# Row sums of 64 MB: seven rows of the last group moved to the head of the load stream

## The chip, the cores and the metric

One core of one Trainium2 chip runs the kernel. The metric is device time in microseconds, the median of several executions. Every execution here is fast, at a granted clock of 1.0. A profile's span is some 2 us shorter than the device time of the same execution, so spans are compared with spans and times with times.

Words and names used below: a load is *issued* when the sync engine starts it and *lands* when the last mark of its completion has come; an instruction that waits for it starts about 0.02 us later in these profiles. In the lines shown, DVE is the vector engine and ACT the scalar engine, SPq is the sync engine's queue, TENSOR_REDUCE is a reduction, CUSTOM_DVE_ANT_0 a halving (both are explained with the kernel), and ACTIVATE the sum of one row on ACT.

## The reference

```python
batch, seq, dim = 32, 512, 1024
x = np.random.randn(batch, seq, dim).astype(np.float32)      # 67.1 MB
return np.sum(x, axis=-1).astype(np.float32)                  # 16,384 sums
```

Each of the 16,384 rows of 1,024 numbers is added up. There is one addition for every number read, so the question is how fast 67.1 MB come in, and how little is left to do when the last of them has come.

## The kernel before

The 16,384 rows are laid out as 8 groups of 128 partitions by 16 rows; one group is 8 MB (8 x 2^20 bytes, 8.39 million), 64 KB for each partition. Three buffers of one group rotate. All loads are issued by the sync engine, in order, on one queue. `vec` is one reduction over several rows on the vector engine; `halves` adds the first half of one row to its second half and accumulates the sum, also on the vector engine; `act` sums one row on ACT. `hold` keeps a load from being issued until a given instruction is done; here the load of group 1 waits for the first sum.

```python
last = J // BIG - 1          # 7
FIRST = 4
pieces = (560, 464)
# ... tc.tile_pool(name="in", bufs=3) as inpool; vec, hold, halves, act: cut ...

def rows(t, a, n, j, n_act, pairs=False):      # load n rows, nv on the vector engine, the rest on ACT
    nv = n - n_act
    block = t[:, a * dim : (a + n) * dim].rearrange("p (n d) -> p n d", d=dim)
    load = nc.sync.dma_start(out=block, in_=rows_from(j, n))
    if pairs:
        for q in range(nv):
            sums_of.append(halves(sums[:, j + q : j + q + 1], block[:, q, :]))
    else:
        sums_of.append(vec(sums[:, j : j + nv], block[:, :nv, :]))
    for q in range(nv, n):
        act(sums[:, j + q : j + q + 1], block[:, q, :], dim)
    return load

for g in range(last):
    t = inpool.tile([P, BIG * dim + 4], fp32)
    if g == 0:
        rows(t, 0, FIRST, 0, 0)
        first = sums_of[-1]
        rows(t, FIRST, BIG - FIRST, FIRST, 0)
        continue
    load = rows(t, 0, BIG, g * BIG, BIG // 2 if g == last - 1 else 0)
    if g == 1:
        hold(load, first, "no descriptors of later loads while the first ones start")

t = inpool.tile([P, BIG * dim + 4], fp32)
j = last * BIG
rows(t, 0, 8, j, 4)
rows(t, 8, 5, j + 8, 2, pairs=True)
two = rows(t, 13, 2, j + 13, 1, pairs=True)
a = BIG - 1
# ... the last row: a clear, two loads of 560 and 464 columns, a halving after each ...
```

The sum of the first piece of the last row is put into the tile beside the second piece, so the last halving has 466 numbers left (464, the sum, and a zero).

## Time and profile before

| kernel before | value |
|---|---|
| device time, median of 3 | 161.72 us (161.71 to 161.91) |
| span of the profiled execution | 160.2 us |
| vector engine busy | 120.1 us, 75% |
| ACT busy | 17.3 us, 11% |
| loads in the stream | 13 |
| mean spacing of whole groups' landings | 19.42 us |

The prediction below shows the chain, the stretches and the end. Two more views are wanted. The first is the page's queue part: queue and kind, packets, MB, and the time of the packets as a share of 16 engines' span.

```profile
q1 hardware_dynamic: 2016, 67.12, 97.7%
```

The second view is the timeline of the last 4 us: start, length, engine, line, operation, shapes, and in brackets how long the engine was idle before it and for what.

```profile
154.11 0.69 DVE L145 CUSTOM_DVE_ANT_0 t<-t 128x512 f32<-128x512 f32 x1 [1.68 <-DMA t<-in_x_dram]
...
156.62 0.69 DVE L145 CUSTOM_DVE_ANT_0 t<-t 128x512 f32<-128x512 f32 x1 [0.59 <-DMA t<-in_x_dram]
156.62 1.03 ACT L158 ACTIVATE unread<-t 128x1024 f32<-128x1024 f32 x1 [0.32 <-DMA t<-in_x_dram]
...
157.37 0.45 DVE L145 CUSTOM_DVE_ANT_0 t<-t 128x280 f32<-128x280 f32 x1
...
157.97 0.40 DVE L145 CUSTOM_DVE_ANT_0 t<-t 128x233 f32<-128x233 f32 x1
```

At 156.62 both engines start on the two-row piece, which has just landed, and both have been waiting for it, the vector engine for 0.59 us.

### The profile page before, as it was taken

The numbers are of one execution on the slowest core, as the hardware profiler recorded it, in microseconds if no ns is written. First come the engines' busy times: TensorE is split into PE (matmuls) and PEld (weight loads), VectorE is DVE, ScalarE is ACT, GpSimd is POOL, SyncE is SP. The second block draws the span as 40 slices with busy tenths as digits, with TensorE's granted clock in tenths as the row PEclk, the third lists the DMA queues.
The fourth block names the chain that finished last, engine by engine and source line by source line (L and its number), as shares of the span: only waits on it lengthen the run. The fifth ranks groups of instructions, "written<-read, shape, count | busy, mean of one in ns | idle before, by whom it ended". The sixth has DMA issues, their size and how long they took to land.

```text
span 160.2 us, 125 instructions
## 1 busy us (share of the span) xinstructions
DVE 120.1 (75%) x22; ACT 17.3 (11%) x31; POOL 0.2 (0%) x4
## 2 busy tenths in 40 slices
DVE  0190059960799959999499994999949999497953
ACT  3000000000000000000000000000000000496953
POOL 0000000000000000000000000000000000000000
DMA  7999996996996996989969969969969969899994
GB/s 270 450 479 503 393 524 262 523 523 262 524 523 262 523 524 262 523 360 425 524 262 523 523 262 524 523 262 523 523 262 523 507 278 523 376 409 410 424 382 109
DMA packets 2928, 67.18 MB, mean 419 GB/s; under 512 B 1264, under 2 KB 1392, under 8 KB 1520
## 3 DMA queue, kind: packets, MB, share of 16 engines
q1 hardware_dynamic: 2016, 67.12, 97.7%
q10 hardware_dynamic: 912, 0.06, 0.3%
HBM read 67.11 MB, written 0.07 MB: 419 GB/s over the span
## 4 chain that ended last, share of the span: by engine, by line
DMA 73%; DVE 25%; SPq 1%; issue 0%; DVEq 0%
DMA t<-in_x_dram 73%; DVE sums L131 24%; SPq L170 1%; SPq L211 0%; DVE t L145 0%; DVEq L242 0%
## 5 line engine op out<-in xcount | busy, mean ns | idle before, releaser
L131 DVE TENSOR_REDUCE sums<-t 128x16 f32<-128x16384 f32 (+3 forms) x9 | 116.6, 12953 | 35.9 <-DMA t<-in_x_dram 35.9
L158 ACT ACTIVATE unread<-t 128x1024 f32<-128x1024 f32 x15 | 15.2, 1012 | 139.7 <-DMA t<-in_x_dram 139.7
L145 DVE CUSTOM_DVE_ANT_0 t<-t 128x512 f32<-128x512 f32 (+2 forms) x6 | 3.5, 602 | 2.4 <-DMA t<-in_x_dram 2.3
L158 ACT ACTIVATION_READ_ACCUMULATOR unread<-t 128x1 f32 x15 | 2.8, 187 | 0.0
L158 ACT ACT_TABLE_LOAD x1 | 1.3, 1283 | 0.8 <-PEq L231 0.8
L145 DVE DVE_READ_ACCUMULATOR2_ANT sums<- 128x1 f32 x5 | 0.4, 83 | 0.0
L231 POOL MEMSET const-bfloat16-1.0<- 128x1 bf16 x1 | 0.1, 101 | 0.0
L231 POOL MEMSET const-uint8-127<- 128x1 uint8 x1 | 0.1, 101 | 0.0
L231 POOL MEMSET const-float32-0.0<- 128x1 f32 x1 | 0.1, 98 | 0.2 <-issue 0.2
L231 POOL MEMSET const-float32-1.0<- 128x1 f32 x1 | 0.1, 98 | 0.0
L145 DVE DVE_READ_ACCUMULATOR2_ANT t<- 128x1 f32 x1 | 0.1, 83 | 0.0
L209 DVE MEMSET t<- 128x1 f32 x1 | 0.1, 59 | 0.0
## 6 DMA issues: line engine op xcount, KB each, us to landing
t<-in_x_dram SPq DMA_DIRECT2D x1, 6144.0 KB, 21.0
t<-in_x_dram SPq DMA_DIRECT2D x1, 4096.0 KB, 31.2
t<-in_x_dram SPq DMA_DIRECT2D x1, 2560.0 KB, 37.0
t<-in_x_dram SPq DMA_DIRECT2D x1, 2048.0 KB, 7.2
t<-in_x_dram SPq DMA_DIRECT2D x1, 1024.0 KB, 39.0
t<-in_x_dram SPq DMA_DIRECT2D x1, 280.0 KB, 39.2
t<-in_x_dram SPq DMA_DIRECT2D x1, 232.0 KB, 39.3
t<-in_x_dram SPq DMA_DIRECT2D x6, 41.1
```

The source lines that it names most:

```text
L131: return nc.vector.tensor_reduce(out=dst, in_=src, axis=mybir.AxisListType.X, op=mybir.AluOpType.add)
L145: return nc.vector.tensor_tensor_reduce(out=src[:, :n], in0=src[:, :n], in1=src[:, n:], scale=1.0, scalar=0.0, op0=mybir.AluOpType.add, op ...
L158: nc.scalar.activation(out=unread[:, :n], in_=src, func=mybir.ActivationFunctionType.Copy, accum_out=dst,)
L170: load = nc.sync.dma_start(out=block, in_=rows_from(j, n))
L209: nc.vector.memset(whole[:, width + 1 :], 0.0)
L231: nc = _bacc.Bacc("TRN2", target_bir_lowering=False, num_devices=1)
```

## The change

Before, the last group arrives after everything else, and its 16 rows are worked off in pieces of 8, 5, 2 and 1. The change moves 7 of these rows to the very start of the stream, where the vector engine has nothing to do, and leaves 9 for the end, in pieces of 6, 2 and 1. Group 0 is loaded whole. In group 6, the last whole group, nine rows are halved on the vector engine and seven summed by ACT, instead of eight reduced and eight summed.

```diff
-    FIRST = 4
+    FIRST = 7
...
+        j = last * BIG
+        t = inpool.tile([P, BIG * dim + 4], fp32)
+        rows(t, 0, FIRST, j, 0)
+        first = sums_of[-1]
         for g in range(last):
             t = inpool.tile([P, BIG * dim + 4], fp32)
-            if g == 0:
-                rows(t, 0, FIRST, 0, 0)
-                first = sums_of[-1]
-                rows(t, FIRST, BIG - FIRST, FIRST, 0)
-                continue
-            load = rows(t, 0, BIG, g * BIG, BIG // 2 if g == last - 1 else 0)
+            if g < last - 1:
+                load = rows(t, 0, BIG, g * BIG, 0)
+            else:
+                rows(t, 0, BIG, g * BIG, 7, pairs=True)
             if g == 1:
                 hold(load, first, "no descriptors of later loads while the first ones start")

         t = inpool.tile([P, BIG * dim + 4], fp32)
-        j = last * BIG
-        rows(t, 0, 8, j, 4)
-        rows(t, 8, 5, j + 8, 2, pairs=True)
-        two = rows(t, 13, 2, j + 13, 1, pairs=True)
+        rows(t, FIRST, 6, j + FIRST, 2, pairs=True)
+        two = rows(t, FIRST + 6, 2, j + FIRST + 6, 1, pairs=True)
```

## The prediction

> **What bounds the kernel now.** I read the page's chain of work that ended last first, because it says which engine a saved microsecond must come from.
>
> ```profile
> ## 4 chain that ended last, share of the span: by engine, by line
> DMA 73%; DVE 25%; SPq 1%; issue 0%; DVEq 0%
> ```
>
> 73% is the load stream and 25% is the vector engine. The vector share looks like a second limit, but the chain only runs through the reductions at the points where a later load waits for a buffer (three buffers rotate). Whether that wait stops the stream is read from how evenly the loads land. So the second view is the table by stretches, cut at the moments when each reduction starts, which are the landings. Its columns are the stretch and its length, then busy time and count for the vector engine, ACT and POOL, the clock, the DMA share and GB/s.
>
> ```profile
> 7.25:21.78 14.53, 4.42 (x2) 0.00 (x0) 0.00 (x0) 1.00 1.04 451
> 21.78:41.14 19.36, 12.95 (x2) 0.00 (x0) 0.00 (x0) 1.00 1.00 433
> 41.14:60.49 19.35, 17.22 (x2) 0.00 (x0) 0.00 (x0) 1.00 1.00 434
> 60.49:80.08 19.59, 17.22 (x1) 0.00 (x0) 0.00 (x0) 1.00 1.01 428
> 80.08:99.51 19.43, 17.22 (x2) 0.00 (x0) 0.00 (x0) 1.00 1.00 432
> 99.51:118.91 19.40, 17.22 (x2) 0.00 (x0) 0.00 (x0) 1.00 1.00 432
> 118.91:138.30 19.39, 17.22 (x1) 0.00 (x0) 0.00 (x0) 1.00 0.94 406
> 138.30:148.01 9.71, 8.69 (x1) 8.43 (x16) 0.00 (x0) 1.00 0.96 414
> 148.01:154.11 6.10, 4.42 (x2) 4.27 (x9) 0.00 (x0) 1.00 1.00 430
> 154.11:156.62 2.51, 1.92 (x6) 2.19 (x4) 0.00 (x0) 1.00 0.97 399
> 156.62:157.97 1.35, 1.17 (x5) 1.15 (x2) 0.00 (x0) 1.00 0.65 183
> ```
>
> A whole group is 16 rows on 128 partitions, 8 MB. Six of them land 19.42 us apart on average (116.52 / 6), while the vector engine needs 17.22 us for each and then idles 2.1 to 2.4 us. The stretch is set by the load, not by the reduction, and the DMA share is about 1.00 in all the steady stretches. (Packets are counted where they are recorded, so GB/s in a short stretch is ragged; the landing times are the safer ruler: 8.39 MB in 19.42 us is 432 GB/s.) One row of every partition costs the stream 19.42 / 16 = 1.214 us. The page agrees from another side: its queue part gives the load queue 97.7% of 16 engines' span.
>
> Third, the end, from the chain in order of time (start, length, what) and from the costliest groups:
>
> ```profile
> 118.59 39.34 DMA t<-in_x_dram
> 157.93 0.05 issue
> 157.97 0.40 DVE t L145
> ```
>
> The last piece lands at 157.93; after it come one short halving-and-adding instruction of 0.40 us and the 8 KB store (issued at 158.41, landing 1.4 us later), and the span ends at 160.2. So span = landing of the last piece + about 2.3 us. Time can only change through that landing, or through work not being ready when the last piece lands.
>
> **What the Trainium skill says.** "DMA: Bandwidth & Descriptors", section "Bandwidth", has 425 GB/s for a 16 MB load by one core alone and derives a ceiling of about 435 GB/s from the 16 ports. The trace has 432 GB/s over the whole groups, which agrees: the stream has almost no headroom, so a reordering of the same bytes can't speed it up. "Perfetto Trace Analysis", section "Identifying the Most-Contended Engine", says to optimise the most contended engine first; here that is the DMA, and this change takes no byte from it. "VectorE: DVE Perf Modes", section on the TRN2 errata, gives (N+151)/0.96 ns for an fp32 two-input operation: N = 512 makes 691 ns, and the trace has 690 ns for the halving instruction. Its tier table has the reduction at one element a cycle; the trace shows 17,220 ns for 16,384 elements, 1.05 ns each, which agrees. Halving reads two elements a step, so a row costs about 0.615 us between starts (154.11, 154.72, 155.34) where the reduction takes 1.08 us.
>
> **The change part by part.**
>
> *The loads.* Before, 13 loads: 4 rows, 12 rows, six groups, 8 rows, 5, 2, and the last row as 560 and 464 columns. After, 12 loads: 7 rows of the last group, seven groups, 6 rows, 2 rows, and the same two pieces. The bytes are the same. From row 13 of the last group onward nothing changes, so what counts is when the first 125 rows have landed (154.11 before). What does one load fewer save? Worked out from the table: the 5-row load took 6.10 us where 5 x 1.214 = 6.07, so 0.03 extra; the 2-row load 2.51 against 2.43, so 0.08 extra; the 8-row load 9.71 against 9.71, nothing. Estimate: 0 to 0.08, say 0.04 us less.
>
> *The start.* Four rows landed at 7.25, of which 4 x 1.214 = 4.86 is transfer and 2.39 is start. Seven rows should land at 7.25 + 3 x 1.214 = 10.9. The vector engine takes about 7 x 1.08 = 7.6 us, so it is done at 18.5. The second group's load is held for that sum (before, for the 4-row sum at 11.68). Meanwhile the first whole group, already queued (its issue was at 0.78 before), lands at 10.9 + 19.42 = 30.3. The held loads thus arrive 11.8 us before the queue runs dry. Cost 0.
>
> *The buffers.* There are nine tiles instead of eight. The first tile's buffer takes group 2 at 18.5, the next frees at 30.3 + 17.2 = 47.5 and takes group 3, while group 1 lands at 49.7 and group 2 is queued whole. That is the steady state of before: a load is issued about 2 us plus a whole group ahead. Cost 0. The small last loads wait for group 4 (landing 108.0, summed by 125.2) and are issued about 21 us before group 6 has landed. Cost 0.
>
> *Group 6.* It should land at 10.9 + 7 x 19.42 = 146.8 (rounded down by the saved load). It was 8 rows for each engine; now nine rows are halvings on the vector engine, 9 x 0.615 = 5.6 us, done at 152.4, and seven are ACT's, at 1.04 us from start to start (138.30, 139.35, 140.39), 7.3 plus a read of 0.1, done at about 154.2.
>
> *The tail.* The six rows land at 154.07. Vector: four halvings, 4 x 0.615 = 2.46, so 156.54 (before: three, done at 156.03). ACT: starts at 154.2 instead of 154.1, two rows, done by 156.4. The two-row piece lands at about 156.58. So the vector engine is free 0.04 us before it rather than 0.59, and ACT about 0.2 before it rather than 0.32. Then halving, clear and the 280-wide halving run to about 157.8 as before, and the last piece lands at 157.9. About 0.1 us of slack stays.
>
> Sum: -0.04 (one load less) + 0 (start, buffers) + 0 (tail) = -0.04 us. The vector engine's 10.1 us of idle time before its second reduction gets shorter, but it is no saving: the stream doesn't wait for it.
>
> **The rivals.**
>
> *The tail becomes compute-bound.* The balance at 154 to 157 is within 0.1 us on both engines. If group 6's seven ACT rows or the four halvings run later than I put them, the last halving starts late. For: the slack shrinks from 0.59 to about 0.04 us. Against: what is late must then eat the further 0.1 us before the last piece. It would make the time 161.7 to 162.0.
>
> *The stream starves early.* With only seven rows in the first buffer the depth of prefetch is smaller, 39 rows instead of 48 before the first buffer comes free, and the hold lasts 7 us longer. For: the chain of before goes through that hold (7.25 to 11.68). Against: 11.8 us of queued data at that moment. If it did starve, the cost would be a start of around 2 us, time 163.5 to 164.
>
> *The stream itself is uneven.* One group of before took 19.59 where the others took 19.35 to 19.43. If that is chance, it adds or takes 0.2 us; if larger first packets (28 KB a partition instead of 16) start faster or slower, another 0.1 or 0.2. That would give 161.4 to 161.9.
>
> *A real gain.* It would need fewer bytes, a shorter start or a shorter end. The end keeps its 2.3 us and the start its 2.4 us; I see no source for more than 0.3 us.
>
> **Range and chances.** The centre is 161.72 - 0.04, rounded to 161.7. Repeats of before spread over 161.71 to 161.91; with the unevenness of a group the 8-in-10 range is 161.3 to 162.0. Two per cent is 3.2 us: 158.5 or 165.0. Nothing above reaches either, the starving rival being the only one that comes near. So faster 0.01, same 0.98, slower 0.01.
>
> **What would show it right or wrong.** Right: the first reduction, 7 rows wide, starts near 10.9; reductions of whole groups start 19.4 us apart from 30.3 on, with about 2 us of vector idle before each; group 6's work starts near 146.8; the last halving still starts because the last piece landed, near 157.9, and takes 0.40 us; the load queue stays at 97 to 98%. Wrong by the tail: the last halving starts right behind the 280-wide one with no wait for a load, or ACT is still in group 6's rows well after 154.2. Wrong by starvation: one interval between landings of about 21 us or more, at group 1 or 2, and a dip in the DMA row there. Wrong in the start: the first landing off 10.9 by more than 0.2.

## More of the kernel before

The sync engine's queue carries the loads, and its packets can be counted by the loads that made them. A load of n rows gives each of 128 partitions one contiguous run, so 128 packets whatever n is. With 16 more for the marks of its end, which is inferred from the counts, 13 loads and one store make 14 x 144 = 2016.

## The result, and the profile after

| | before | after |
|---|---|---|
| device time, median of 6 | 161.81 us (161.68 to 162.12) | 161.74 us (161.62 to 162.10) |
| span of the profiled execution | 160.2 us | 159.9 us |
| vector engine busy | 120.1 us | 120.6 us |
| ACT busy | 17.3 us | 11.9 us |
| loads | 13 | 12 |

The ratio is 0.9997, with a 95% interval of 0.9983 to 1.0011. Ratios here are the mean time of one kernel's fast runs over that of the other's of the same rounds, so not quite the ratio of the medians. The two kernels are equally fast.

The chain of the changed kernel by engine:

```profile
DMA 71%; DVE 27%; SPq 1%; issue 0%; DVEq 0%
```

Its load queue:

```profile
q1 hardware_dynamic: 1872, 67.12, 97.5%
```

The chain is made of the same parts as before. The queue has 144 packets fewer, just one load (128 runs and 16 ends), and is busy for the same share of the span.

The stretches between landings, cut as before (columns as in the prediction):

```profile
11.08:30.38 19.30, 7.62 (x1) 0.00 (x0) 0.00 (x0) 1.00 1.00 435
30.38:49.74 19.36, 17.22 (x1) 0.00 (x0) 0.00 (x0) 1.00 1.00 433
49.74:69.09 19.35, 17.22 (x1) 0.00 (x0) 0.00 (x0) 1.00 1.00 434
...
127.14:146.50 19.36, 17.22 (x2) 0.00 (x1) 0.00 (x0) 1.00 0.93 401
146.50:153.80 7.30, 5.60 (x18) 7.30 (x14) 0.00 (x0) 1.00 0.99 426
153.80:156.29 2.49, 2.49 (x8) 2.19 (x5) 0.00 (x0) 1.00 0.99 401
156.29:157.64 1.35, 1.17 (x7) 1.15 (x2) 0.00 (x0) 1.00 0.56 158
```

The stream still sets the pace: 19.35 us for a group and 17.22 us of reduction in it. New are the full columns near the end: from 146.50 to 153.80 ACT is busy all 7.30 us, and from 153.80 to 156.29 the vector engine all 2.49 us. The timeline of the last 4 us shows the same:

```profile
153.80 0.69 DVE L145 CUSTOM_DVE_ANT_0 t<-t 128x512 f32<-128x512 f32 x1 [1.70 <-DMA t<-in_x_dram]
...
156.29 1.03 ACT L158 ACTIVATE unread<-t 128x1024 f32<-128x1024 f32 x1 [0.31 <-DMA t<-in_x_dram]
156.30 0.69 DVE L145 CUSTOM_DVE_ANT_0 t<-t 128x512 f32<-128x512 f32 x1
...
157.04 0.45 DVE L145 CUSTOM_DVE_ANT_0 t<-t 128x280 f32<-128x280 f32 x1
...
157.64 0.40 DVE L145 CUSTOM_DVE_ANT_0 t<-t 128x233 f32<-128x233 f32 x1
```

The two-row piece has landed by 156.29, where ACT starts with it. The vector engine comes to it at 156.30 without having waited: its 0.59 us of idle time before this piece are gone, spent on the fourth halving, and it is just not late. From the piece to the last halving both kernels take 1.35 us.

The last halving starts 0.33 us earlier in this profile than in the one before, though the times differ by 0.07 us. The profiled execution of before was one of 162.02 us, that of after one of 161.70, each with its own scatter: in the first, groups are 19.35 to 19.59 us apart, in the second 19.30 to 19.36. The longer stretches come in the changed kernel too: a later execution of it (e11, below) has 19.75 and 19.52. There the last halving starts at 158.11, later than in the kernel before. So the 0.33 us is for the most part not the change's.

### The profile page after: what moved, and what is told of

Read it like the earlier page. It is cut to its first block, busy times and chain, and to the rows that moved or that the text cites. A ratio compares the mean times of both kernels' runs of the same rounds, so it can differ in the third digit from the quotient of the medians.

```text
span 159.9 us, 132 instructions
## 1 busy us (share of the span) xinstructions
DVE 120.6 (75%) x40; ACT 11.9 (7%) x21; POOL 0.2 (0%) x4
## 3 DMA queue, kind: packets, MB, share of 16 engines
q1 hardware_dynamic: 1872, 67.12, 97.5%
## 4 chain that ended last, share of the span: by engine, by line
DMA 71%; DVE 27%; SPq 1%; issue 0%; DVEq 0%
DMA t<-in_x_dram 71%; DVE sums L131 26%; SPq L170 0%; SPq L212 0%; DVE t L145 0%; DVEq L243 0%
## 5 line engine op out<-in xcount | busy, mean ns | idle before, releaser
L131 DVE TENSOR_REDUCE sums<-t 128x16 f32<-128x16384 f32 (+1 forms) x7 | 110.9, 15849 | 33.4 <-DMA t<-in_x_dram 33.4
L158 ACT ACTIVATE unread<-t 128x1024 f32<-128x1024 f32 x10 | 10.1, 1013 | 144.7 <-DMA t<-in_x_dram 144.7
L145 DVE CUSTOM_DVE_ANT_0 t<-t 128x512 f32<-128x512 f32 (+2 forms) x16 | 9.6, 657 | 4.0 <-DMA t<-in_x_dram 3.8
L158 ACT ACTIVATION_READ_ACCUMULATOR unread<-t 128x1 f32 x10 | 1.9, 187 | 0.0
L145 DVE DVE_READ_ACCUMULATOR2_ANT sums<- 128x1 f32 x15 | 1.3, 84 | 0.0
```

The costliest lines, as they stand in the source:

```text
L131: return nc.vector.tensor_reduce(out=dst, in_=src, axis=mybir.AxisListType.X, op=mybir.AluOpType.add)
L145: return nc.vector.tensor_tensor_reduce(out=src[:, :n], in0=src[:, :n], in1=src[:, n:], scale=1.0, scalar=0.0, op0=mybir.AluOpType.add, op ...
L158: nc.scalar.activation(out=unread[:, :n], in_=src, func=mybir.ActivationFunctionType.Copy, accum_out=dst,)
```

## The experiments

The theory is that the stream of loads sets the time of both kernels, so that nothing counts but the number of contiguous runs it is cut into, whether it runs dry, and what is left when it ends. There are three rivals: the new tail is limited by the engines, the shallower start lets the stream run dry, or an earlier start of the vector engine is a gain. Each experiment was run beside the kernel before on the same chip.

### e1: group 6 with a reduction again

```diff
-                rows(t, 0, BIG, g * BIG, 7, pairs=True)
+                rows(t, 0, BIG, g * BIG, 7)
```

> The changed kernel with the nine vector rows of group 6 summed by one reduction instead of nine halvings (loads unchanged). Theory (the tail of the changed kernel has only about 0.1 to 0.2 us of slack, and the halvings in group 6 are what keeps it): the reduction takes 9 x 1.08 = 9.7 us, so from 146.5 it ends at 156.2 instead of 152.1; the four halvings of the six-row piece then start 2.4 us after their landing, and the last halving starts near 159.8 instead of 157.64 with no wait for a load. Time +2.2 us, about 163.9. Rival (the tail has room, halving in group 6 was not needed): under +0.5 us.

Measured: 164.10 us, ratio 1.013 (1.011 to 1.0149), so +2.1 us. The timeline:

```profile
146.69 9.76 DVE L131 TENSOR_REDUCE sums<-t 128x9 f32<-128x9216 f32 x1 [2.15 <-DMA t<-in_x_dram]
156.36 0.68 DVE L145 CUSTOM_DVE_ANT_0 t<-t 128x512 f32<-128x512 f32 x1
...
160.03 0.40 DVE L145 CUSTOM_DVE_ANT_0 t<-t 128x233 f32<-128x233 f32 x1
```

No halving after the reduction has a bracket: none waited for a load, the vector engine is the bound from here to the end. So the move of the rows needs the halvings (the halvings without the move were not run). Moving seven rows to the front takes 7 x 1.21 = 8.5 us of stream away from behind group 6, in which the engines could catch up with it; the cheaper halvings in group 6 make that good.

### e5: one more halving in the tail

```diff
-        rows(t, FIRST, 6, j + FIRST, 2, pairs=True)
+        rows(t, FIRST, 6, j + FIRST, 1, pairs=True)
```

> The changed kernel with five of the six rows of the six-row piece halved on the vector engine and one summed by ACT, instead of four and two. Theory (slack of the tail is what lies between the 280-wide halving and the last one, about 0.15 to 0.2 us in the changed kernel): the fifth halving makes the vector engine 0.6 us late for the two-row piece, the last halving starts right behind the 280-wide one, and the time goes up by 0.6 less that slack, about +0.4 us (162.1 to 162.2). Rival (more slack than that): no change.

Measured: 162.32 us, ratio 1.0024 (1.0006 to 1.0042); against the changed kernel's ratio of 0.9997 that is +0.27% or 0.4 us. The two intervals still overlap, so the trace counts for more:

```profile
156.39 1.03 ACT L158 ACTIVATE unread<-t 128x1024 f32<-128x1024 f32 x1 [1.35 <-DMA t<-in_x_dram]
156.96 0.69 DVE L145 CUSTOM_DVE_ANT_0 t<-t 128x512 f32<-128x512 f32 x1
...
157.58 0.45 DVE L145 CUSTOM_DVE_ANT_0 t<-t 128x280 f32<-128x280 f32 x1
...
158.18 0.40 DVE L145 CUSTOM_DVE_ANT_0 t<-t 128x233 f32<-128x233 f32 x1
```

The two-row piece landed at 156.39 (ACT), the vector engine came to it 0.57 us late. From the landing to the last halving it now takes 158.18 - 156.39 = 1.79 us instead of 1.35. So 0.44 of the 0.57 us came through and the slack is 0.13 us. Where that is I had put wrongly in the expectation. Between the starts of the 280-wide and the last halving there are 0.60 us here, as in both kernels and in e1, where nothing was waited for: that is the vector engine's own time, and in both kernels the last piece lands just before it is over (157.59 for a start at 157.64 after the change). What shrinks is the stretch ahead of it, from the two-row halving to the 280-wide one: 0.74 us in the changed kernel (156.30 to 157.04), where the first piece of the last row lands at 157.0 and is waited for, against 0.62 us in this run, where it has landed at 157.1 and the halving starts at 157.58.

### e2 and e7: what a load, or a run, costs the stream

e2 cuts each whole group into four loads of four rows:

```diff
-        def rows(t, a, n, j, n_act, pairs=False):
+        def rows(t, a, n, j, n_act, pairs=False, parts=1):
...
-            load = nc.sync.dma_start(out=block, in_=rows_from(j, n))
+            m = n // parts
+            loads = [
+                nc.sync.dma_start(out=block[:, k * m : (k + 1) * m, :], in_=rows_from(j + k * m, m))
+                for k in range(parts)
+            ]
+            load = loads[0]
...
-                load = rows(t, 0, BIG, g * BIG, 0)
+                load = rows(t, 0, BIG, g * BIG, 0, parts=4)
...
-                rows(t, 0, BIG, g * BIG, 7, pairs=True)
+                rows(t, 0, BIG, g * BIG, 7, pairs=True, parts=4)
```

> The changed kernel with each of the seven whole groups loaded by four loads of four rows instead of one of sixteen (33 loads instead of 12), reductions unchanged. Theory (each load has a fixed cost of about 0.04 us in the full stream, from which the prediction got its -0.04): whole groups land 19.35 + 3 x 0.04 = 19.47 us apart, time +0.84 us, about 162.6. Rival (a load costs the full stream nothing, the small surpluses of the last loads are an end effect): 19.35 us apart, time unchanged within 0.2 us. If a load costs as the two-row load seemed to, 0.08, it is 19.59 apart and +1.7 us.

e7 keeps one load for each of groups 0 to 5, but leaves a gap of 32 bytes in the tile after every four rows, so that a partition is again written in four runs of 16 KB:

```diff
+    GAPPED = 4 * dim + 8
...
+        def rows_in_runs(t, j):
+            quads = t[:, : 4 * GAPPED].rearrange("p (k w) -> p k w", w=GAPPED)[:, :, : 4 * dim]
+            load = nc.sync.dma_start(
+                out=quads, in_=rows_from(j, BIG).rearrange("p (k n) d -> p k (n d)", k=4)
+            )
...
-                load = rows(t, 0, BIG, g * BIG, 0)
+                load = rows_in_runs(t, g * BIG)
```

Cut here are the one reduction over all 16 rows, which reads around the gaps, and the tiles' size, now `4 * GAPPED`.

> The changed kernel with groups 0 to 5 each loaded by one load whose every partition is written in four runs of 16 KB with gaps between them (as many pieces as with four loads to a group, but one load, one completion). It tells what the 0.07 us for each extra load was. Theory (the cost is that of a load, its completion): groups land 19.35 us apart, time as the changed kernel. Rival (the cost is that of the shorter runs, 24 more for each engine in a group, about 9 ns each): 19.56 apart, time +1.3 us.

Measured: e2 163.68 us, ratio 1.0107 (1.0089 to 1.0126); e7 162.85 us, 1.0055 (1.0037 to 1.0073). The load queue of e2, and two landings in its timeline:

```profile
q1 hardware_dynamic: 4896, 67.12, 98.0%
```

```profile
30.72 17.22 DVE L131 TENSOR_REDUCE sums<-t 128x16 f32<-128x16384 f32 x1 [12.03 <-DMA t<-in_x_dram]
...
128.51 17.22 DVE L131 TENSOR_REDUCE sums<-t 128x16 f32<-128x16384 f32 x1 [2.25 <-DMA t<-in_x_dram]
```

The same two views of e7:

```profile
q1 hardware_dynamic: 4176, 67.12, 97.9%
```

```profile
30.64 17.22 DVE L132 TENSOR_REDUCE sums<-t 128x16 f32<-128x16384 f32 x1 [11.93 <-DMA t<-in_x_dram]
...
128.44 17.22 DVE L132 TENSOR_REDUCE sums<-t 128x16 f32<-128x16384 f32 x1 [2.39 <-DMA t<-in_x_dram]
```

Five groups take 97.79 us in e2 and 97.80 in e7, 19.56 each, where the changed kernel has (127.14 - 30.38) / 5 = 19.35. Packets confirm that e7 has the runs without the loads: 4176 - 1872 = 2304 = 6 groups x 384 runs. So my theory for e7 fell: it is the runs that cost, not the completions. 24 more for each of the 16 engines in a group (384 spread evenly) cost 0.21 us, about 8.7 ns each. The times agree as far as their intervals go: against the changed kernel's ratio, e2 is 1.8 us slower and e7 0.9, where seven groups at 0.21 make 1.5 and six make 1.3. By the times alone a run would cost 10.6 ns in e2 and 6.5 ns in e7, so the figure is good to a third or so. One load fewer is 8 runs fewer for each engine. If runs of other lengths cost the same, that saves an estimated 0.07 us (0.05 to 0.09), which no time here can show.

The Trainium skill has a number of this size: "DMA: Bandwidth & Descriptors", section "Bandwidth", gives about 10.5 ns a packet as the floor of very small transfers. It is no confirmation: it divides the 0.67 us of a lone 4 KB transfer by 64 packets, while the 8.7 ns are what one more run of 16 KB costs one engine in a full stream.

### e3: no hold

```diff
-            if g == 1:
-                hold(load, first, "no descriptors of later loads while the first ones start")
```

The hold orders two loads that share no data, so taking it away leaves no race.

> The changed kernel without the order that holds the load of group 1 until the first seven rows are summed. Theory (queue depth is ample: the held load comes 11.7 us before the queue runs dry): time unchanged within 0.2 us, first landing at 11.1 and the groups 19.35 us apart as before. Rival 1 (the hold costs something at the start): the landings of groups 0 and 1 come earlier, time down by up to 0.3 us. Rival 2 (descriptors of the later load disturb the first ones, as the kernel's comment has it): first landing later than 11.1, time up.

Measured: 161.87 us, ratio 0.9997 (0.9976 to 1.0017), first landing at 11.08 as with the hold. In the changed kernel no cost and no help of the hold is seen, to within 0.2%. It ends at 18.7, when the queued group 0 still has 11.7 us to go.

### e4: two buffers

```diff
-        tc.tile_pool(name="in", bufs=3) as inpool,
+        tc.tile_pool(name="in", bufs=2) as inpool,
```

> The changed kernel with two input buffers instead of three. Theory (the stream only needs the next load to be issued before the one under way has landed; a reduction ends 2.13 us before the next landing, and from issue to first packets took about 1.0 us at the start): groups still land 19.35 us apart, time within 0.3 us of the changed kernel. Rival (the smaller depth starves the stream, as the rival of the prediction had it for the first tile): every group lands later by what is missing, for a latency of 3 us 0.9 us each over six groups, time +5 us or more.

Measured: 168.83 us, ratio 1.0412 (1.0369 to 1.0456). The theory's claim fell, the rival was right. The timeline of the vector engine:

```profile
49.66 17.22 DVE L131 TENSOR_REDUCE sums<-t 128x16 f32<-128x16384 f32 x1 [2.12 <-DMA t<-in_x_dram]
70.38 17.22 DVE L131 TENSOR_REDUCE sums<-t 128x16 f32<-128x16384 f32 x1 [3.50 <-DMA t<-in_x_dram]
90.36 17.22 DVE L131 TENSOR_REDUCE sums<-t 128x16 f32<-128x16384 f32 x1 [2.76 <-DMA t<-in_x_dram]
110.74 17.22 DVE L131 TENSOR_REDUCE sums<-t 128x16 f32<-128x16384 f32 x1 [3.16 <-DMA t<-in_x_dram]
132.22 17.22 DVE L131 TENSOR_REDUCE sums<-t 128x16 f32<-128x16384 f32 x1 [4.25 <-DMA t<-in_x_dram]
```

The brackets are the tell-tale: 2.1 us of idle time where the stream is full, up to 4.25 us here. The load of group 2 was issued at 47.56, 2.1 us before group 1 had landed at 49.66, and landed 22.8 us later, 3.5 us more than a group's transfer of 19.35. So 2.1 us of queued work was not enough to keep the stream full; the intervals are 20.0 to 21.5 us. More was not safe either: the load issued at 107.61 had 3.1 us in front of it and lost 2.1 us (110.74 to 132.22 are 21.48), the next had 4.2 us and lost 0.8. How many microseconds are queued is not the whole rule; e10 comes back to this. The prediction's rival of a starving stream is real, then. It just does not apply to three buffers, where a whole group lies in between.

### e6, e12, e9 and e10: the kernel before with a larger first load

e6 makes the first load 7 rows instead of 4, so that the second has 9:

```diff
-    FIRST = 4
+    FIRST = 7
```

> The kernel before with a first load of 7 rows instead of 4 (the second then 9 instead of 12), nothing else. Theory (the first load's start is fixed and its size is worth nothing): first landing near 11.0, group 0 complete near 21.8, time as before within 0.2 us. Rival (larger first runs of 28 KB a partition start later, which would explain 11.08 where 10.9 was predicted): first landing at 11.1 again and everything after it 0.15 us later than in the kernel before.

Measured: 162.42 us, ratio 1.0026 (1.0007 to 1.0046). The first landing was at 10.97, but the kernel was 0.4 us slower, which neither had foreseen. The rival of a later start is not settled by this landing alone, since e12, the same kernel, has 11.10. Against it speaks e10, whose eight rows land at 11.96, earlier than the 12.10 that the start of the kernel before and eight rows make (2.39 + 8 x 1.214), and e9, which keeps the seven rows and shows no loss. The hold is a suspect: with 7 rows it ends at 18.6, and the nine rows behind the first load have landed by 21.9, so only 3.3 us are queued. e9 is e6 without the hold (its diff is that of e3):

> The kernel before with a first load of 7 rows and without the hold of group 1's load. With the hold this kernel ran 0.26% (0.4 us) slower than the kernel before, which neither theory had foreseen. Theory (the hold ends at 18.6, when only 3.3 us of queued data are left, and with two buffers a load issued into a nearly empty queue took 3.5 to 5.3 us more than its transfer): without the hold the time is back to that of the kernel before within 0.15 us. Rival (the 0.4 us was scatter, or comes from the first load's size): as slow as with the hold, +0.4 us, or both the same as before within the interval.

Measured: 161.87 us, ratio 0.9992 (0.9969 to 1.0016), so back, and group 1 lands 19.35 us after group 0:

```profile
22.02 9.75 DVE L131 TENSOR_REDUCE sums<-t 128x9 f32<-128x9216 f32 x1 [3.36 <-DMA t<-in_x_dram]
41.37 17.22 DVE L131 TENSOR_REDUCE sums<-t 128x16 f32<-128x16384 f32 x1 [9.59 <-DMA t<-in_x_dram]
```

e10 keeps the hold and has `FIRST = 8`, so that about 1.0 us is left in the queue:

> The kernel before with a first load of 8 rows and the hold kept. The hold then ends near 12.2 + 8.7 = 20.9, when about 1.0 us of queued data is left (group 0 complete near 21.9). Theory (a load needs some 3.5 to 5.3 us from issue to a running stream, as with two buffers): the landing of group 1 comes 2.5 to 4.3 us later than 41.2, time +2.5 to +4 us. Rival (the start of a load costs only the 2.6 us that the very first one took): +1.6 us.

Measured: 163.38 us, ratio 1.0088 (1.006 to 1.0116), so +1.4 us. That is less than I expected and near the rival's 1.6. The timeline of the vector engine:

```profile
21.66 8.69 DVE L131 TENSOR_REDUCE sums<-t 128x8 f32<-128x8192 f32 x1 [1.01 <-DMA t<-in_x_dram]
42.35 17.22 DVE L131 TENSOR_REDUCE sums<-t 128x16 f32<-128x16384 f32 x1 [12.01 <-DMA t<-in_x_dram]
```

Group 1 lands 20.69 us after group 0, 1.34 more than 19.35. e12 is e6 once more, since e6 rested on one session:

> The kernel before with a first load of 7 rows and the hold kept, a second time, because its 0.4 us rested on one session and its profile happened to be of the fastest of its six runs. Theory (the hold that ends with 3.3 us of queued data left costs something in some executions): again slower than the kernel before by 0.2 to 0.5 us, and if the profile falls in such an execution, the stretch from group 0 to group 1 is longer than 19.6 us. Rival (scatter): within 0.15 us of the kernel before.

Measured: 162.31 us, ratio 1.0026 (1.0006 to 1.0046), the same again, and the profile points to the step from group 0 to group 1:

```profile
22.10 9.75 DVE L131 TENSOR_REDUCE sums<-t 128x9 f32<-128x9216 f32 x1 [3.38 <-DMA t<-in_x_dram]
41.73 17.22 DVE L131 TENSOR_REDUCE sums<-t 128x16 f32<-128x16384 f32 x1 [9.88 <-DMA t<-in_x_dram]
```

It is 19.63 us, 0.3 more than a full stream. One stretch of that length proves little (e9, without the hold, has one of 19.58), but the five that follow in e12 are 19.33 to 19.37. So the hold costs about 0.4 us with 3.3 us queued (two sessions against e9; the intervals of e6, e12 and e9 still touch), 1.4 us with 1.0 us, and nothing that is seen with 11.7. This answers why the changed kernel can afford a first load of 7 rows: it puts a whole group behind it, not the nine rows left over.

From issue to landing, a load took 2.3 us more than its transfer in e10 but 3.5 us and more in e4, although e4 had more queued. The kept traces hold the time of each of a load's 16 completion marks (`prof` prints only the landing, which is the last), and they tell why. In the changed kernel the 16 marks of a load come within 0.6 us. In e4 they spread to 3.1 us: of the load issued at 107.61, twelve have come by 129.36 and the last comes at 132.20. In e12 only one mark of group 1 is late, at 41.71 after 41.13 for the fifteenth. Take the ninth mark instead of the last, for what was queued and for the loss, which is the step between the ninth marks of two groups less 19.35 us. Then the loss follows what was queued: none for 2.7 to 3.0 us (e4, e6, e12), 0.5 and 0.9 us for 1.8 us, 1.1 and 1.2 us for 1.3 to 1.4 us (all e4), 1.3 us for 0.8 us (e10). The rest of the loss in e4, and the 0.3 us in e12, is a few marks that come late. Why they do is not shown.

### e8: no early start at all

The kernel before with group 0 loaded whole and no hold:

```diff
-            if g == 0:
-                rows(t, 0, FIRST, 0, 0)
-                first = sums_of[-1]
-                rows(t, FIRST, BIG - FIRST, FIRST, 0)
-                continue
-            load = rows(t, 0, BIG, g * BIG, BIG // 2 if g == last - 1 else 0)
-            if g == 1:
-                hold(load, first, "no descriptors of later loads while the first ones start")
+            rows(t, 0, BIG, g * BIG, BIG // 2 if g == last - 1 else 0)
```

> The kernel before with group 0 loaded whole by one load of 16 rows, and without the hold, which would now wait for the whole group's sum. The vector engine then starts at about 21.7 instead of 7.25, with one load less. Theory (the early start of the vector engine is worth nothing, a load less saves 0.04 to 0.08 us): groups land 19.35 to 19.42 apart from 21.7 on, time as before within 0.2 us, at best 0.1 lower. Rival (the early small load buys time, by starting the vector engine early and so freeing buffers early): time up by 0.5 us or more.

Measured: 162.07 us, ratio 1.001 (0.9993 to 1.0028). The first reduction:

```profile
21.95 17.22 DVE L131 TENSOR_REDUCE sums<-t 128x16 f32<-128x16384 f32 x1 [21.95 <-DMA t<-in_x_dram]
```

The vector engine starts at 21.95 instead of 7.25, and no loss is seen; the interval leaves room for at most 0.45 us, which rules out the rival. So there is no sign that it is worth anything to fill this early time of the vector engine, as the change does.

### e11: the changed kernel again

> The changed kernel itself, on the chip of these runs, to have it beside them and to narrow its interval. Theory (8 runs fewer for each engine at 8.75 ns, worked out from the two experiments that cut groups into 16 KB runs): 0.07 us lower than the kernel before, interval including 1. Landings of groups 19.35 to 19.45 us apart.

Measured: 161.71 us, ratio 0.9987 (0.9964 to 1.001). With the first result of 0.9997 that agrees with a gain of 0.07 us (0.04%), with none, and with one of a few tenths; executions of one kernel with three buffers on one chip differ by up to 1 us, so it can't be settled at this size. Its profile has the longer stretches named above:

```profile
49.66 17.22 DVE L131 TENSOR_REDUCE sums<-t 128x16 f32<-128x16384 f32 x1 [2.13 <-DMA t<-in_x_dram]
69.41 17.22 DVE L131 TENSOR_REDUCE sums<-t 128x16 f32<-128x16384 f32 x1 [2.53 <-DMA t<-in_x_dram]
88.93 17.22 DVE L131 TENSOR_REDUCE sums<-t 128x16 f32<-128x16384 f32 x1 [2.31 <-DMA t<-in_x_dram]
```

No experiment pointed to a version that beats both kernels.

## Why the prediction was right

The predicted 161.7 us was measured as 161.74. That the two agree to 0.04 us is luck, since executions of one kernel differ by up to 1 us; that nothing clear of noise would change is what the prediction earned. Its steps one by one:

- **The stream is the bound.** Right: whole groups land 19.35 us apart with 2.1 us of vector idle time before each, and the load queue stays at 97.5%. e1 and e4 show what it looks like when it is not so.
- **One load less saves 0.04 us (0 to 0.08).** Plausible in sign and probably small: e2 and e7 give an estimate of 0.07 us, inside the range stated; the difference itself was never measured clear of noise. Part of the gap is that I took the surplus of single loads off a mean spacing of 19.42 that contained scatter: with 19.35 for 16 rows, the loads of 5, 2 and 8 rows have 0.05, 0.09 and 0.03 us extra. The kind was wrong: the term belongs to the contiguous runs and not to the load.
- **The start costs nothing.** Nothing to the contrary is seen, by e3 and e8. The first landing was put at 10.9; all eleven profiles with seven rows first have 10.97 to 11.10, which is 0.1 to 0.2 late. The 2.39 us for the start came from one profile of four rows. A start that grows with the load doesn't fit e10, which puts it at about 2.3 us for eight rows. The cause stays open, and 0.1 us is as large as the saving predicted.
- **The buffers cost nothing.** Right within the noise (e3), with 11.7 us queued when the hold ends. e4, e10 and e12 show the cost on the other side of the line.
- **Group 6 and the tail.** Right in order and nearly in time: ACT through with group 6's rows at 153.89 (put at 154.2), the vector engine at the two-row piece with about no idle time left (put at 0.04 us). The slack, put at about 0.1 us, is 0.13 us by e5, but for another reason, so that the agreement is luck. The prediction took it to lie between the end of the 280-wide halving (157.8) and the last landing (157.9). Yet from the start of that halving the vector engine needs 0.60 us of its own before the last one starts, in e1 and e5 too, and that is over when the last piece lands. So the statement that the last halving waits for the last piece is half right at best: the landing of the piece before it, for which the 280-wide halving waits, sets the time just as much.
- **The uneven stream as a rival.** This is what the 0.33 us between the two profiles mostly is, as e11 shows.

## What to carry to other kernels

Where a stream of loads is full, putting the same bytes in another order moves work between idle places and saves only what the stream itself sheds, here an estimated 8 runs at 8.7 ns for each engine. Before making use of idle time at the start, ask whether anything waits for it; before taking away a late piece, ask which engine caught up during it. And a wait that delays a load should first be judged by how many microseconds of transfer are still queued when it ends: 11.7 were ample here, while 1.0 to 4.2 us lost up to 2.1 us, and not in order of size.

## What the Trainium skill lacked or had wrong

- "DMA: Bandwidth & Descriptors", section "Bandwidth": its 425 GB/s were measured with loads issued from GpSimd. Loads issued by the sync engine, one core alone, sustain 8.39 MB in 19.35 us, 434 GB/s, closer to the 435 it derives.
- The same section treats the cost of a packet or descriptor for small ones only, and gives no figure for long runs. Runs of 16 KB instead of 64 KB still cost: about 8.7 ns for each more on an engine, 0.21 us in 19.35 for a group.
- The same page, section "Rules for kernel authors", says to issue a load early but not how early. Here 11.7 us of queued transfer was enough, 3.3 us cost 0.4 us and 1.0 us cost 1.4 us; with two buffers, 2.1 us left in front of group 2's load cost 1.4 us, and 2.7 to 4.2 us before later loads cost 0.6 to 2.1 us.
- No page mentions scatter from run length. Four executions each of e2 and e7, with runs of 16 KB, lay within 0.09 and 0.04 us; the kernels with 64 KB runs and three buffers scattered by 0.2 to 1.0 us. The cause was not tried, and four executions on one chip are few.
